# A hybrid decoder layer on one core: gate pieces as tiles of their own, activations behind the high parts, the residual scaled on another engine, 44 ups ahead

## The chip, the core and the metric
The kernel runs on one core of one Trainium2 chip. A time is that of one execution on the device in microseconds; several runs are given by their median. Engines are PE (matrix), DVE (vector), ACT (scalar), POOL (GpSimd) and SP, which only issues transfers here. Each has its own queue and works through it in order.

## What is computed
For 256 tokens of width 2048 (and 16 meta tokens ahead of them, whose output is dropped):
```python
h = layer_norm(concat(meta, x))
proj = h @ w_in                                  # 2048 x 8192
ya = (pool_scale * grouped(multiscale_pool(a), pool_w)) @ pool_proj
yb = (zb * causal_conv(zc * zh)) @ conv_proj
h = layer_norm(ALPHA * h + (g0 * ya + g1 * yb) @ w_out)
q = h @ w_q                                      # 8 heads, two halves of 128
# per head: top 16 of each half's 128 scores, top 16 of their sums -> 16 expert numbers, softmax gate
act = gelu(h . expert_u[idx]);  y = sum(gate * act * expert_v[idx])
out = layer_norm(ALPHA * h + y)
```
There are 16384 experts, 128 blocks of 128. All is float32.

## The kernel before
**Products.** A float32 product is made of rounded parts: `hi`, the value cast to the matrix format, and `lo`, the rest. For each 128x1024 half of a weight tile ACT casts the high part (`whi`, line 95) and DVE or POOL subtracts for the low part (`wlo`, line 74, called by `halves`). PE multiplies the high part with both parts of the tokens and the low part with the high part only (lines 108 and 109, in `mm2`). Weights come in 1 MB tiles named `raw` (line 84), three of them in turn, all issued on SP; the parts have three buffers each.

**Stages.** (1) Layer norm and transposes. (2) Input projection: 64 weight tiles, among them a loop over 8 chunks of the convolution (lines 299 to 320), three tiles a round. In round 1 the residual `res` is scaled by the input norm's row and shifted (lines 319 and 320); it is first read again after the output projection. (3) Output projection, second norm, queries; `q_done` finds the top scores on DVE. (4) The experts are not gathered for the first 224 tokens (`TD`). All 128 blocks are multiplied through instead: an *up* (`up`) multiplies one block of `expert_u` with all tokens and leaves 128 experts x 224 tokens, to which Gelu is applied (line 620); `coef` multiplies it by the gates `G` (line 642), zero for experts not chosen; a *down* (`down`) multiplies the coefficients of four blocks by half the columns of `expert_v` (line 654) and adds to `res` (line 663). The last 32 tokens gather their rows by indirect transfers (`lone_rows`, tile `lone`), a step now and then (a *tick* is half an up or one block of a down).

**Lead.** The first `LEAD` ups run before any down, while the routing ends: `finish(t)` is queued after ups 3 and 6 (`ROUTED`) and goes on by one `yield` per half up; it has the softmax's Exp (line 521). From up 10 on `gates()` builds the gates: a step takes 8 tokens (`GT`), compares indices on DVE (lines 573 to 581), multiplies 16 small matrices on PE (line 592), and ACT copies the result into `wide` (line 594); four steps make a group of 32 tokens (`TG`), which is written to a DRAM tile `spill` (line 597) from POOL's queue. There are 7 groups and 29 calls, spread evenly by `rate` per half up, ending four ups (by the formula) ahead of the lead's end. `G` for four blocks is read back from `spill` for all groups: for the first two fours in `gates` (line 600), for the others by `fetch` (line 738), two slots in turn.

**Order.** The text is not the order on the engines. A planner goes through the program with estimated durations and writes each engine's queue: an engine that is free in its plan takes, of the instructions that are ready in the plan, the one that stands earliest in the text. `tc.high_priority(offset=n)` puts an instruction n places earlier (the parts of weight halves, lines 94 to 98); `tc.issue_after(i)` puts what is issued in its block on the engine of `i` behind `i` in that engine's queue. `late` lets that many Gelus stand back in the text (`gelus`, line 617).

Of the kernel before, what the change touches and what calls it, by code (L numbers as in the profile page):

```python
# [8 lines left out]
F32 = mybir.dt.float32  # L9
# [9 lines left out]
P = 128  # L19
# [19 lines left out]
UAHEAD = 100  # L39
LEAD = 36  # L40
ROUTED = (3, 6)
# [12 lines left out]
def block(ctx, tc, x, meta, w_in, small, pool_w, projs, w_out, wq, keys, eu, eur, ev,  # L54
# [35 lines left out]
    def halves(parts, raw, lo_eng=None, lo_eng1=None, ahead=AHEAD):  # L90
        for s in range(2):
            hi = parts.tile([P, 1024], F32R, name="whi")
            lo = parts.tile([P, 1024], F32R, name="wlo")
            with tc.high_priority(offset=ahead):
                nc.scalar.copy(hi, raw[:, s])  # L95
                eng = lo_eng1 if s and lo_eng1 else lo_eng
                last_lo[0] = lo_part(lo, raw[:, s], hi, eng)
                last_on["pool" if eng is nc.gpsimd else "dve"] = last_lo[0].ins
            yield hi, lo
# [70 lines left out]
    with ExitStack() as pa:  # L170
# [128 lines left out]
        for c in range(NCH):  # L299
            zh = a2.tile([P, T + 2], F32, name="zh", bufs=1)  # L300
            nc.scalar.copy(zh, in_tile(META - 2))
            z = a2.tile([P, T + 2], F32, name="z", bufs=1)
            nc.vector.tensor_tensor(z, in_tile(META - 2), zh, op=OP.mult)
            cv = a2.tile([P, T], F32, name="cv", bufs=1)
            nc.vector.tensor_scalar(cv, z[:, 0:T], conv_w[:, 0, c:c + 1], conv_b[:, c:c + 1],
                                    op0=OP.mult, op1=OP.add)
            for k in (1, 2):
                nc.vector.scalar_tensor_tensor(cv, z[:, k:T + k], conv_w[:, k, c:c + 1], cv,
                                               op0=OP.mult, op1=OP.add)
            zb = a2.tile([P, T], F32, name="zb", bufs=1)  # L310
            both(zb, in_tile(META), T)
            nc.vector.tensor_tensor(cv, zb, cv, op=OP.mult)
            split(yb[:, c, 0], yb[:, c, 1], cv)
            if c == 1:
                with tc.issue_after(last_load[0]):
                    bcast_row(lg, lin_g)
                    bcast_row(lb, lin_b)
                for t in range(NT):
                    nc.gpsimd.tensor_tensor(res[:, t], res[:, t], lg, op=OP.mult)
                    nc.gpsimd.tensor_tensor(res[:, t], res[:, t], lb, op=OP.add)  # L320

# [38 lines left out]
    with ExitStack() as pw:  # L360
# [154 lines left out]
        def finish(t):  # L515
# [3 lines left out]
            for _ in range(3):  # L519
                yield  # L520
            nc.scalar.activation(gt, gt, AF.Exp)
            yield
# [5 lines left out]
            if t == NT - 1:  # L528
# [4 lines left out]
                for n in range(SETS):  # L533
                    hs = slice(n * HEADS // SETS, (n + 1) * HEADS // SETS)
                    to = slice(n * LONE, (n + 1) * LONE)
                    nc.vector.tensor_copy(lone_e[to], rows[ones, hs].rearrange("p h k -> p (h k)"))
                    nc.vector.tensor_copy(lone_g[to], gt[ones, hs].rearrange("p h k -> p (h k)"))
                    nc.sync.dma_start(lone[to], res[ones, t])
            ps = ps_mm()
# [12 lines left out]
    with ExitStack() as pb:  # L552
        lonex = pool(pb, "lonex", 1)
        lone = lonex.tile([P, D], F32, name="lone")
        lone_e = lonex.tile([P, NU], I32, name="lone_e")
# [4 lines left out]
        dram = pb.enter_context(tc.tile_pool(name="dram", bufs=1, space=bass.MemoryType.DRAM))  # L560
        spill = dram.tile([NG, P, NKEY, TG], F32, name="spill")
        p_oh = ExitStack()
# [4 lines left out]
        def gates():  # L567
# [16 lines left out]
            def product(t0, Ag, B):  # L584
# [11 lines left out]
                if o + GT == TG:  # L596
                    nc.gpsimd.dma_start(spill[n], wide[0])
                    for g, eng in ((n - 1, nc.gpsimd), (n if n == NG - 1 else -1, nc.sync)):
                        for b in range(2 if g >= 0 else 0):
                            eng.dma_start(Gs[b][:, g], spill[g, :, b * NB:(b + 1) * NB])  # L600

# [15 lines left out]
        def gelus(left):  # L617
            while len(acts) > left:
                gl = acts.pop(0)
                nc.scalar.activation(gl, gl, AF.Gelu)  # L620

# [114 lines left out]
        def fetch(n):  # L736
            Gs[n] = Gp.tile([P, NG, NB, TG], F32, name="G")
            nc.sync.dma_start(Gs[n], spill[:, :, n * NB:(n + 1) * NB].rearrange("g p i t -> p g i t"))

# [12 lines left out]

        for e in range(LEAD):
            tick(up(e, (nc.gpsimd, nc.gpsimd), UAHEAD, 4 if e <= ROUTED[1] + 2 else 0))
            if e in ROUTED:
                waiting.append(finish(ROUTED.index(e)))
            if e == ROUTED[1] + 3:
                while waiting:
                    step()
                ahead, rate = gates(), (TD // GT + 1) / (2 * (LEAD - 4 - e))  # L760
        for _ in ahead:
            pass
        p_oh.close()
        p_r.close()
        coefp = pool(pb, "coefp", NB + 1)
        lonep = pool(pb, "lonep", 1)
        p_g1 = pb.enter_context(ExitStack())
        rowp = pool(p_g1, "rowp", 2)
# [121 lines left out]
```

## Time and profile before
| | us |
|---|---|
| median of 3 runs (lowest, highest) | 2182.58 (2181.99, 2183.01) |
| profiled execution, its own time | 2188.65 |
| span of the profiled execution | 2186.9 |
| PE busy | 2076.8 |
| DVE, ACT, POOL busy | 1548.2, 1008.9, 586.4 |

PE is busy for 95% of the span, at a mean granted clock of 0.975 (1.00 is the upper of its two levels, 2.4 GHz; the lower is 1.2). The page cuts the span into 40 equal slices of 54.7 us and gives the busy tenths of each. In a row of a window the columns are: from and to, length, and for each engine its busy time and number of instructions, then PE's granted clock, the DMA engines' share and GB/s; PEld is the load of weights, beside PE. A row of a timeline has the start, the duration, the engine, the line, the operation, what is written from what, its shape and count, and in brackets the idle time before it with what ended it. A row of the waits has who waited for whom, the sum, the count and the longest.

### The profile page before, as it was taken

How to read it: one execution, taken by the hardware profiler on the slowest of the kernel's cores; microseconds unless marked ns; L12 is line 12 of the kernel's file. 1: busy time of each engine (PE TensorE's matmuls, PEld its weight loads, DVE VectorE, ACT ScalarE, POOL GpSimd, SP SyncE). 2: the span in 40 equal slices, each digit the busy share in tenths (PEclk: the TensorE clock that was granted, in tenths of full speed). 3: DMA queues.
4: the chain of work that ended last, by engine and by line, in shares of the span. 5: the costliest groups of instructions: out<-in, count | busy, mean ns of one | idle time of the engine just before them, and what ended most of it. 6: DMA issues, size and time to landing. Idle time of an engine off the chain costs nothing.

```text
span 2186.9 us, 29680 instructions
## 1 busy us (share of the span) xinstructions
PE 2076.8 (95%) x11558; PEld 1785.8 (82%) x11558; DVE 1548.2 (71%) x2332; ACT 1008.9 (46%) x1423; POOL 586.4 (27%) x290
## 2 busy tenths in 40 slices
PE   7989999999997787887999999999999999999997
PEld 7989888888886777776888888888888888887775
DVE  7865566666779667755777777776677777678877
ACT  5434545444442454443444444444454444444542
POOL 0110000000073675652323233232333333330001
PEclk9999999999999899898999999999999999999998
DMA  5545555566543345567787877877778787777554
GB/s 196 193 165 183 193 181 187 192 230 229 198 166 122 135 179 199 213 241 245 266 295 260 288 271 265 289 268 285 272 272 284 266 293 261 269 276 250 193 193 154
DMA packets 111452, 498.06 MB, mean 228 GB/s; under 512 B 8320, under 2 KB 35456, under 8 KB 70464
## 3 DMA queue, kind: packets, MB, share of 16 engines
q1 hardware_dynamic: 100704, 413.60, 55.1%
q0 software_dynamic: 10608, 82.58, 9.5%
q8 instruction: 90, 1.47, 0.3%
q14 instruction: 50, 0.41, 0.1%
HBM read 478.32 MB, written 16.78 MB: 226 GB/s over the span
## 4 chain that ended last, share of the span: by engine, by line
PE 55%; DMA 2%; DVE 1%; POOL 0%; issue 0%; ACT 0%; SPq 0%; DVEq 0%; POOLq 0%
PE acc L654 27%; PE mm L108 15%; PE mm L109 7%; PE mm L654 5%; DMA G<-spill 1%; DMA spill<-wide 0%; DVE gl L642 0%; POOL wlo L74 0%; PE mm L592 0%; DVE res L806 0%; DVE res L805 0%; DVE st L140 0%; DVE res L663 0%; ACT whi L95 0%; DVE c_lo L74 0%
## 5 line engine op out<-in xcount | busy, mean ns | idle before, releaser
L95 ACT CAST whi<-raw 128x1024 fp32r<-128x1024 f32 x738 | 771.6, 1048 | 707.1 <-PE mm L108 258.8
L74 DVE TENSOR_TENSOR wlo<-raw,whi 128x1024 fp32r<-128x1024 f32 x554 | 689.6, 1249 | 422.8 <-ACT whi L95 418.4
L108 PE MATMUL mm<-x_hl,whi 128*128 128x448 f32 x2048 | 670.9, 384 | 21.3 <-ACT whi L95 21.3
L74 POOL TENSOR_TENSOR wlo<-raw,whi 128x1024 fp32r<-128x1024 f32 x184 | 463.2, 2525 | 679.5 <-ACT whi L95 344.6
L109 PE MATMUL mm<-x_hl,wlo 128*128 128x224 f32 x2048 | 551.1, 269 | 43.0 <-POOL wlo L74 34.3
L109 PEld LDWEIGHTS mm<-x_hl,wlo 128*128 128x128 f32 x2048 | 401.3, 196 | 49.3 <-POOL wlo L74 38.0
L108 PEld LDWEIGHTS mm<-x_hl,whi 128*128 128x128 f32 x2048 | 394.8, 193 | 56.1 <-ACT whi L95 22.4
L654 PE MATMUL acc<-wlo,c_hi 128*128 128x512 f32 (+1 forms) x864 | 270.2, 394 | 9.5 <-DVE wlo L74 9.5
L654 PE MATMUL acc<-whi,c_lo 128*128 128x512 f32 (+1 forms) x864 | 270.2, 394 | 0.0
L654 PE MATMUL acc<-whi,c_hi 128*128 128x512 f32 (+1 forms) x864 | 269.5, 393 | 0.0
L108 PE MATMUL mm<-h_hl,whi 128*128 128x512 f32 x640 | 226.7, 397 | 0.0
L654 PEld LDWEIGHTS acc<-wlo,c_hi 128*128 128x128 f32 (+1 forms) x864 | 151.0, 175 | 57.7 <-DVE wlo L74 9.9
L654 PEld LDWEIGHTS acc<-whi,c_lo 128*128 128x128 f32 (+1 forms) x864 | 151.5, 175 | 48.4
L109 PE MATMUL mm<-h_hl,wlo 128*128 128x256 f32 x640 | 181.3, 283 | 5.5 <-DVE wlo L74 5.5
L654 PEld LDWEIGHTS acc<-whi,c_hi 128*128 128x128 f32 (+1 forms) x864 | 147.7, 175 | 44.5
L136 POOL TENSOR_TENSOR rstd<-rstd,neghalf 128x1 f32<-128x1 f32 (+1 forms) x7 | 5.8, 826 | 659.3 <-DVE rstd L135 659.3
L663 DVE SCALAR_TENSOR_TENSOR res<-res,acc 128x512 f32<-128x512 f32 x216 | 136.9, 681 | 31.4 <-PE acc L654 28.6
L620 ACT ACTIVATE gl<-gl 128x224 f32<-128x224 f32 x128 | 50.1, 392 | 234.2 <-DVE gl L113 234.2
L108 PEld LDWEIGHTS mm<-h_hl,whi 128*128 128x128 f32 x640 | 121.2, 189 | 27.7
L109 PEld LDWEIGHTS mm<-h_hl,wlo 128*128 128x128 f32 x640 | 121.8, 190 | 5.8 <-DVE wlo L74 5.8
L104 PE MATMUL mm<-h_hl,wlo 128*128 128x258 f32 (+3 forms) x384 | 110.1, 287 | 4.1 <-DVE wlo L74 4.1
L103 PE MATMUL mm<-h_hl,whi 128*128 128x258 f32 (+3 forms) x384 | 111.5, 291 | 0.0
(189 smaller groups left out, 2573.0 us busy)
## 6 DMA issues: line engine op xcount, KB each, us to landing
raw<-in_eu SPq DMA_DIRECT2D x128, 1024.0 KB, 4.9
raw<-in_ev SPq DMA_DIRECT2D x128, 1024.0 KB, 5.4
raw<-in_w_in SPq DMA_DIRECT2D x64, 1024.0 KB, 5.4
raw<-in_projs SPq DMA_DIRECT2D x16, 1024.0 KB, 6.4
raw<-in_w_out SPq DMA_DIRECT2D x16, 1024.0 KB, 5.4
raw<-in_wq SPq DMA_DIRECT2D x16, 1024.0 KB, 4.9
spill<-wide POOLq DMA_DIRECT2D x7, 2048.0 KB, 9.4
G<-spill SPq DMA_DIRECT2D x30, 448.0 KB, 6.7
```

What stands on the lines that cost most here:

```text
L74: return (eng or nc.vector).tensor_tensor(lo, full, hi.bitcast(F32), op=OP.subtract)
L95: nc.scalar.copy(hi, raw[:, s])
L103: nc.tensor.matmul(ps, whi, xlo, start=False, stop=False)
L104: nc.tensor.matmul(ps, wlo, xhi, start=False, stop=last)
L108: nc.tensor.matmul(ps[:, :2 * n].rearrange("p (s t) -> p s t", s=2), whi, xhl, start=first, stop=False)
L109: nc.tensor.matmul(ps[:, :n], wlo, xhl[:, 0], start=False, stop=last)
L136: nc.gpsimd.tensor_tensor(r[:n], r[:n], neghalf[:n], op=OP.pow)
L620: nc.scalar.activation(gl, gl, AF.Gelu)
L654: nc.tensor.matmul(ps[c][:n_t], c_[:, ts], v_[:, c * 512:(c + 1) * 512], start=e == first and n == 0, stop=e == last and n == 2)
L663: nc.vector.scalar_tensor_tensor(r, r, 1.0 if (t, dh, c) in added else ALPHA, ps[c][:n_t], op0=OP.mult, op1=OP.add)
```

## The change
Five things are changed. The DVE scales `res`, in 8 pieces of 512 columns over rounds 1 to 7 instead of four passes of POOL in round 1; the two rows for it are loaded one round earlier. Exp and each Gelu are queued behind the newest high part on ACT, and 3 Gelus stand back through the whole lead. `spill` becomes seven DRAM tiles; in `gates` the reads of a group are queued behind the put of the next; a `fetch` is seven transfers. The lead is 44 ups and the gates end seven ups (by the formula) ahead of its end. `lone` is filled after the lead, from the same rows of `res`, and its tile is made there.
```diff
-LEAD = 36
+LEAD = 44
@@ halves
-                nc.scalar.copy(hi, raw[:, s])
+                last_on["act"] = nc.scalar.copy(hi, raw[:, s]).ins
@@ convolution loop
-            if c == 1:
+            if c == 0:
                 with tc.issue_after(last_load[0]):
                     bcast_row(lg, lin_g)
                     bcast_row(lb, lin_b)
-                for t in range(NT):
-                    nc.gpsimd.tensor_tensor(res[:, t], res[:, t], lg, op=OP.mult)
-                    nc.gpsimd.tensor_tensor(res[:, t], res[:, t], lb, op=OP.add)
+            else:
+                for n in range(8 * (c - 1) // 7, 8 * c // 7):
+                    q = slice(n % 4 * 512, (n % 4 + 1) * 512)
+                    r = res[:, n // 4, q]
+                    with tc.issue_after(last_on["dve"]):
+                        nc.vector.tensor_tensor(r, r, lg[:, q], op=OP.mult)
+                        nc.vector.tensor_tensor(r, r, lb[:, q], op=OP.add)
@@ finish
-            nc.scalar.activation(gt, gt, AF.Exp)
+            with tc.issue_after(last_on["act"]):
+                nc.scalar.activation(gt, gt, AF.Exp)
...
-                    nc.sync.dma_start(lone[to], res[ones, t])
@@ the experts' tiles
-        lone = lonex.tile([P, D], F32, name="lone")
-        spill = dram.tile([NG, P, NKEY, TG], F32, name="spill")
+        spill = [dram.tile([P, NKEY, TG], F32, name=f"spill{n}") for n in range(NG)]
@@ gates
-                    nc.gpsimd.dma_start(spill[n], wide[0])
-                    for g, eng in ((n - 1, nc.gpsimd), (n if n == NG - 1 else -1, nc.sync)):
-                        for b in range(2 if g >= 0 else 0):
-                            eng.dma_start(Gs[b][:, g], spill[g, :, b * NB:(b + 1) * NB])
+                    put = nc.gpsimd.dma_start(spill[n], wide[0])
+                    with tc.issue_after(put.ins):
+                        for g, eng in ((n - 1, nc.gpsimd), (n if n == NG - 1 else -1, nc.sync)):
+                            for b in range(2 if g >= 0 else 0):
+                                eng.dma_start(Gs[b][:, g], spill[g][:, b * NB:(b + 1) * NB])
@@ gelus
-                nc.scalar.activation(gl, gl, AF.Gelu)
+                with tc.issue_after(last_on["act"]):
+                    nc.scalar.activation(gl, gl, AF.Gelu)
@@ fetch
-            nc.sync.dma_start(Gs[n], spill[:, :, n * NB:(n + 1) * NB].rearrange("g p i t -> p g i t"))
+            for g in range(NG):
+                nc.sync.dma_start(Gs[n][:, g], spill[g][:, n * NB:(n + 1) * NB])
@@ the lead
-            tick(up(e, (nc.gpsimd, nc.gpsimd), UAHEAD, 4 if e <= ROUTED[1] + 2 else 0))
+            tick(up(e, (nc.gpsimd, nc.gpsimd), UAHEAD, 3))
...
-                ahead, rate = gates(), (TD // GT + 1) / (2 * (LEAD - 4 - e))
+                ahead, rate = gates(), (TD // GT + 1) / (2 * (LEAD - 7 - e))
         for _ in ahead:
             pass
+        gelus(0)
...
         lonep = pool(pb, "lonep", 1)
+        lone = lonep.tile([P, D], F32, name="lone")
+        for n in range(SETS):
+            nc.sync.dma_start(lone[n * LONE:(n + 1) * LONE], res[P - LONE:, NT - 1])
```

## Rows read from the trace of the kernel before

**Rows 1.** The page's 40 slices of the span: busy tenths of PE.
```profile
PE   7989999999997787887999999999999999999997
```
**Rows 2.** Windows of five stretches, all engines.
```profile
100.00:125.00 25.00, 15.39 (x88) 14.15 (x88) 23.54 (x10) 4.71 (x7) 18.55 (x4) 0.80 0.33 119
150.00:300.00 150.00, 150.00 (x992) 137.73 (x991) 88.51 (x116) 68.85 (x96) 0.00 (x0) 1.00 0.54 185
812.00:970.00 158.00, 130.66 (x966) 120.90 (x964) 106.37 (x168) 73.09 (x122) 102.40 (x58) 0.89 0.59 209
1050.00:1950.00 900.00, 900.00 (x4777) 765.22 (x4776) 649.08 (x769) 433.16 (x599) 293.28 (x142) 1.00 0.78 277
2000.00:2050.00 50.00, 50.00 (x219) 37.92 (x218) 42.89 (x49) 25.73 (x29) 1.44 (x1) 1.00 0.61 207
```
**Rows 3.** Windows, line 109 alone (one per pair of an up): PE, PEld, clock.
```profile
688.00:742.00 54.00, 23.25 (x79) 17.52 (x79) 0.78 0.34 103
740.00:755.00 15.00, 12.34 (x47) 8.90 (x48) 1.00 0.65 218
700.00:790.00 90.00, 48.08 (x170) 35.60 (x170) 0.83 0.39 129
812.00:970.00 158.00, 85.31 (x301) 63.21 (x302) 0.89 0.59 209
970.00:1010.40 40.40, 15.61 (x52) 11.73 (x51) 0.80 0.74 244
```
**Rows 4.** Windows, line 592 alone (matmuls of gate steps): PE, PEld, clock.
```profile
812.00:970.00 158.00, 26.33 (x363) 22.39 (x360) 0.89 0.59 209
```
**Rows 5.** Timeline of POOL and DVE, 99 to 130 us.
```profile
99.13 9.28 POOL L319 TENSOR_TENSOR res<-res,lng 128x2048 f32<-128x2048 f32 x2 [84.16 <-DVE ya L74]
99.46 4.54 DVE L312 TENSOR_TENSOR cv<-zb,cv 128x256 f32<-128x256 f32 x1
...
125.40 1.23 DVE L74 TENSOR_TENSOR wlo<-raw,whi 128x1024 fp32r<-128x1024 f32 x1 [1.79 <-ACT whi L95]
129.79 0.42 DVE L312 TENSOR_TENSOR cv<-zb,cv 128x256 f32<-128x256 f32 x1
```
**Rows 6.** Timeline of ACT, 690 to 800 us: Exp and one Gelu.
```profile
710.16 0.31 ACT L521 ACTIVATE gt<-gt 128x128 f32<-128x128 f32 x1 [15.50 <-DVE gt L518]
...
768.54 0.39 ACT L620 ACTIVATE gl<-gl 128x224 f32<-128x224 f32 x1 [8.61 <-DVE gl L113]
```
**Rows 7.** Timeline of DVE: the adds that empty the first ups' banks.
```profile
713.90 0.38 DVE L113 TENSOR_TENSOR gl<-gl,mm 128x224 f32<-128x224 f32 x1
...
727.51 0.38 DVE L113 TENSOR_TENSOR gl<-gl,mm 128x224 f32<-128x224 f32 x1
...
734.96 0.39 DVE L113 TENSOR_TENSOR gl<-gl,mm 128x224 f32<-128x224 f32 x1
```
**Rows 8.** Waits of the whole span.
```profile
POOL G L600 <- DMA spill<-wide: 41.1, 6, 9.4
```
**Rows 9.** Timeline of POOL: low parts of ups, and reads of gates.
```profile
736.78 19.24 POOL L74 TENSOR_TENSOR wlo<-raw,whi 128x1024 fp32r<-128x1024 f32 x8 [2.46 <-ACT whi L95]
...
948.86 1.11 POOL L600 DMA_DIRECT2D G<-spill  x2 [5.23 <-DMA spill<-wide]
```
**Rows 10.** Timeline of DVE, 940 to 1045 us: first and last run-ahead multiplies.
```profile
973.96 1.90 DVE L642 TENSOR_TENSOR gl<-gl,G 128x224 f32<-128x224 f32 x6 [6.28 <-DMA G<-spill]
...
1007.91 1.30 DVE L642 TENSOR_TENSOR gl<-gl,G 128x224 f32<-128x224 f32 x4 [7.23 <-DMA G<-spill]
```
**Rows 11.** DMA issues: engine, count, KB each, median us to landing.
```profile
G<-spill SPq DMA_DIRECT2D x30, 448.0 KB, 6.7
...
G<-spill POOLq DMA_DIRECT2D x12, 64.0 KB, 2.1
```
**Rows 12.** Timeline of SP in the main loop: a fetch and the next loads.
```profile
1289.87 0.38 SPq L738 DMA_DIRECT2D G<-spill  x1
1291.93 7.28 SPq L84 DMA_DIRECT2D raw<-in_ev  x2
```

## The prediction

> **What bounds the kernel now.** I read the page's slices first: PE is at nine tenths or more almost everywhere, with dents in slices 1 (the start, which the change leaves alone), 3 and 13 to 19 [rows 1]. The windows then say how full PE is where there is no dent: 900.00 of 900 us between 1050 and 1950, at full clock [rows 2]. Nothing that the change does there can give time; it can only take some. So the time to be had is what is lost in the dents, 700 to 1010 us above all, and I size it by counting work. An up is 16 pairs of matmuls (high, then low part); undisturbed, 47 to 48 pairs take 15.0 us [rows 3], so a pair is 0.314 us and an up 5.0 us. A gate step is 16 small matmuls, 0.88 us at full clock by my estimate (0.055 us each, their start distance). Elapsed time less work at that speed is the loss, idle time and low clock together:
> - 700 to 790: 170 pairs are 53.4 us, with 2 us of transposes and first gate products; 34 us lost.
> - 812 to 970: 301 pairs (94.5) and 363 gate matmuls (20.0) [rows 3, 4]; 43 us lost.
> - 970 to 1010.4: 52 pairs (16.3); 24 us lost.
> - 100 to 125: 15.39 of 25 us busy, so 9.6 idle, and the granted clock of 0.80 means 10 us at the lower level, 1.2 GHz [rows 2]. Part of those 10 us is idle anyway, so the clock costs at most 5; I take 3. Together 12.6 us.
> The sum is 114 us, the most that the change can win.
>
> **Residual on DVE.** Before, POOL scales res in four 128x2048 passes, two of them 9.28 us, and is busy 18.55 of these 25 us; a DVE operation beside them takes 4.54 us that alone takes 0.42 [rows 2, 5]. The low parts come late and PE waits. The change takes POOL out of this: 12.6 us back. It adds 16 DVE operations of 128x512. A 128x1024 one takes 1.23 us [rows 5], so about 0.61 each, 9.8 us, over seven rounds of the convolution loop. They are hidden by DVE's own idle time, 61 us between 150 and 300 [rows 2], and stand behind the newest low part, so they delay the next one by 1.2 us at most. Without that cover they cost 9.8 us; below zero they can't go. I take 0. The two row loads go to SP one round earlier, same number, same bytes.
>
> **Exp and Gelu behind the high parts.** ACT is a queue: at 694 it reaches Exp, waits 15.50 us for DVE, and all high parts of the next ups wait behind it; the Gelu at 768.54 does the same for 8.61 us [rows 6]. Now Exp stands behind the high parts of the up traced last (the sixth), and each Gelu behind those of an up three later. The wait itself stays: DVE is late. What is late next is the add that empties an up's PSUM bank, at 713.90, 727.51 and 734.96 for the first three ups [rows 7], and there are four banks. So ups 0 to 3 run through; up 4 starts at about 714.3; up 5 waits for the second add, and its high part also for the Gelu of up 1, which is queued in front of it: 727.9 + 0.4 Gelu + 1.05 high part, so it ends near 735.5; up 6 follows the third add and ends at about 742. That is 7 ups by 742, against 79 pairs, 4.9 ups, before [rows 3]: 10 us. The later stall at 768 (about 8 us) goes, since no high part stands behind a young Gelu any more and two ups fit into the 12 us for which DVE is late. I take 18 of the 34 us. Bounds: 5 (only Exp moves, DVE's adds come later still) and 30 (DVE's adds come earlier in the new order).
>
> **Gate pieces.** POOL puts a group of 32 tokens to the spill, then comes to the reads of the same group and waits until the write has landed, 41.1 us in 6 waits, 9.4 the longest; the row at 948.86 shows one [rows 8, 9]. The low parts of the ups queue behind it. With separate tiles, and the reads behind the next put, a read finds its write landed four steps earlier. The two reads take POOL 1.11 us [rows 9], the put by estimate half of that, 1.7 us per four steps in all. Is another engine late next? The rate falls from 29/46 to 29/56 step per half up, so a step has 1.93 x 2.5 + 0.88 = 5.7 us of PE instead of 4.85. DVE was busy 106.4 us for 22.7 steps, 4.7 each with the adds [rows 2, 4]: 83%. POOL needs 1.93 low parts of 2.4 us (19.24 for 8 [rows 9]) and 0.4: 5.1 us, 89%. Both fit. Of the 43 us I take 39; bounds 25 (POOL's 1.7 us burst shows each time and the last write still blocks SP) and 43.
>
> **Transition and the 44 ups.** When the gates are done, DVE runs ahead: it multiplies all waiting Gelus by their gates, group after group, each group's G fetched by SP into two slots. First multiply 973.96, last of nine groups 1007.91: 34 us [rows 10], and the low parts that the next ups and the first down need on DVE stand between and behind them. That is the 24 us. After, the gates end 6 ups before the lead's end and not 3, so 15 us more of ups, whose low parts are all on POOL, run beside the chain. But 44 ups are eleven groups, and two more cost 34/7 = 4.9 us each. Loss 24 - 15 = 9 if nine groups stand ahead of the first low part on DVE, 19 if eleven: I take 13, a gain of 11; bounds -5 and 21. The eight lead ups have both low parts on POOL, 4.8 of 5.0 us: no cost, and 1.6 us if each of the 16 stretches by a tenth. The four lone loads move from the routing (SP has the same issues there and here) to this place, behind the release of the gate tiles; they are needed only by the first gathered row, so 0, and 5 us if SP is held by them.
>
> A fetch is now seven issues of 64 KB instead of one of 448 KB. The single one lands in 6.7 us, a 64 KB read from POOL in 2.1 [rows 11]. If the seven overlap, a fetch takes 7 x 0.38 + 2.1 = 4.8 us; one after another, 14.7. I keep 6.7, between them, for the chain. The Trainium skill (DMA: Bandwidth & Descriptors, Anatomy of one DMA) gives each DMA on the POOL path a fixed 2.0 us and a part that goes with the bytes, and puts most of the fixed part down to the receipt of the write; by that the pieces overlap, 64 KB is 2.15 us (the trace: 2.1) and 448 KB only 3.0, where the trace has 6.7; by its figures the sum below would come out some 7 us lower. In the main loop the fetch is 2.26 us more of SP per group. SP issues a fetch at 1289.87 and then waits until 1291.93 for a raw slot [rows 12], so 1.7 us of it fit into that wait and the rest into the lead of three raw tiles: 0.
>
> The lone rows take as many ticks as before; 64 of them now lie in the downs-only end, where DVE is busy 42.89 of 50 us with PE at 50.00 [rows 2]: 0.
>
> **Sum.** 12.6 + 18 + 39 + 11 = 80.6, say 81 us. The profiled execution took 2188.65 us (span 2186.9), 6 us over the median of the runs; from its time 2107.6, and by the same difference 2182.58 - 81 = 2101.6 as the median. About 0.2%, 4.4 us, is what a measurement can tell from no change.
>
> **Rivals.**
> - Nearly all of it goes (0.20): DVE's adds are placed earlier, the chain overlaps. 12.6 + 26 + 42 + 21 = 102: 2081. For it: DVE has idle time in the new gate stage. Against: the adds at 727.51 and 734.96 are late by DVE's own queue, with no idle time ahead of them [rows 7], whatever ACT does.
> - The pieces land one after another in the chain (0.15). 8 us more per fetch, two in flight, so 4 more per group; seven groups 62 us instead of 34; the transition loses 44 instead of 24: 12.6 + 18 + 39 - 20 = 50: 2133. The Trainium skill's fixed price per DMA (same page and section) speaks for it, if it is paid in turn. Against: the two POOL reads of a group are issued side by side and still land in 2.1 us [rows 11].
> - The reads still wait (0.07), because what they wait for is not the tile but the queue's newest write: 12.6 + 18 + 0 + 11 = 42: 2141. For it: the wait named in the rows is the write. Against: it is the write of the same group.
> - Slower (0.05): the pieces land in turn in the main loop too, and hold back the raw loads behind them in SP's queue. 30 fetches x (8 - 1.7 - c), where c is how early raw tiles lie ready. With c = 3 that is 99 us, against 50 won: 2232. It decides from c = 4.6 us. Against: PE is full for 900 us with no wait on a raw load, and three tiles are in flight.
> - My forecast: 0.53.
>
> The range holds the forecast, the first rival and most of the second: 2073 to 2138, with 2 in 10 outside. Faster by over 0.2%: all but the slower rival and a little of the third's tail, 0.94; within 0.2% 0.01; slower 0.05.
>
> **What would show it.** Right: 100 to 125 at PE 25 of 25; no POOL wait on the spill between 800 and 980 and PE over 0.95 there; ACT still waiting for DVE near 715 to 735, but no wait of Exp over 2 us; a stall of 10 to 20 us once, at the first main-loop up, with DVE waiting for G; from there PE full. Wrong: PE idle in the main loop behind a raw load; low parts on POOL late after each put; a transition as long as before; or DVE full through the gate stage.

## The result and the profile after

The changed kernel takes 2130.34 us (median of 4 runs, 2129.3 to 2131.58) beside 2182.8 us for the one before (2181.99 to 2183.15, same chip): a ratio of 0.976, 95% interval 0.9744 to 0.9777. The forecast was 2101.6 us; the gain is 52 us where 81 were forecast, and the time lies in the range, 8 us under its upper end. The profiled execution took 2131.58 us (span 2129.8, mean granted clock 0.986).

The page's slices of PE show what is left of the dents in [rows 1]:
```profile
PE   7999999999999699997999999999999999999997
```
Counted from 1, slices 3, 13 and 15 to 18 are at nine tenths or more now; a slice is 53.2 us long. Two dents remain, slice 14 (692 to 745 us) and slice 19 (958 to 1012). The windows size them (columns as in the windows of before):
```profile
100.00:150.00 50.00, 50.00 (x373) 47.93 (x372) 33.06 (x43) 20.65 (x27) 0.00 (x0) 1.00 0.52 180
...
690.00:700.00 10.00, 3.32 (x22) 2.92 (x20) 10.00 (x22) 2.34 (x2) 4.20 (x2) 0.82 0.62 211
700.00:710.00 10.00, 2.53 (x9) 2.39 (x10) 10.00 (x60) 1.57 (x3) 1.24 (x1) 0.50 0.01 2
...
765.00:938.00 173.00, 173.00 (x1384) 163.51 (x1383) 133.77 (x212) 101.32 (x170) 146.74 (x76) 1.00 0.74 268
938.00:1016.00 78.00, 57.33 (x277) 49.15 (x276) 42.52 (x75) 26.52 (x42) 28.30 (x13) 0.85 0.75 234
...
1100.00:1700.00 600.00, 600.00 (x3180) 509.70 (x3179) 431.85 (x522) 289.33 (x402) 195.51 (x94) 1.00 0.79 277
```
The stretch in which POOL scaled the residual before [rows 2] and the stretch of the gates (765 to 938) are full at clock 1.00, and so is the main loop. In the first dent it is DVE that is busy without a gap (10.00 of 10, twice) while PE stands. To count work as before, the windows of line 109 alone:
```profile
690.00:765.00 75.00, 42.31 (x151) 31.48 (x151) 0.84 0.39 133
765.00:938.00 173.00, 122.78 (x468) 88.98 (x467) 1.00 0.74 268
938.00:1016.00 78.00, 32.90 (x114) 24.50 (x113) 0.85 0.75 234
```
At 0.314 us a pair, 0.055 us a gate matmul (448 of them from 765 to 938) and 0.23 us a matmul of a down (50 from 938 to 1016), the losses are:

| stretch | before, us lost | after, us lost | gain | forecast |
|---|---|---|---|---|
| residual (100 to 125; first up starts 674.3, was 688.0) | 12.6 | about 0 | 13.7 | 12.6 |
| routing (before 700 to 790, after 690 to 765) | 34 | 75 - 47.4 - 1.4 = 26 | 8 | 18 |
| gates (before 812 to 970, after 765 to 938) | 43 | 173 - 147.0 - 24.6 = 1 | 42 | 39 |
| transition (before 970 to 1016, after 938 to 1016) | 46 - 16.3 - 4.4 = 25.3 | 78 - 35.8 - 11.5 = 30.7 | -5.4 | 11 |

The 1.4 us are transposes. The gains add up to 58, where the two profiled executions differ by 57.1 (2188.65 and 2131.58). The medians differ by 52.5, 4.6 less: the profiled execution of before lay 6 us over its median, this one 1.2. The forecast took a gain counted in the profiled execution from the median of the runs.

The waits show the change of the limits. PE, 650 to 765 us, and DVE, 930 to 1016 us (who waited for whom, sum, count, longest):
```profile
PE mm L108 <- DVE gl L113: 16.6, 2, 14.1
```
```profile
DVE gl L647 <- DMA G<-spill: 38.0, 9, 8.9
```
No wait of POOL for a write of the spill, 41.1 us before [rows 8], is left between 765 and 938. The timeline of ACT from 690 to 765 us and that of DVE's adds that empty the banks answer to [rows 6, 7]:
```profile
707.36 0.39 ACT L625 ACTIVATE gl<-gl 128x224 f32<-128x224 f32 x1 [14.19 <-DVE gl L113]
...
724.61 0.31 ACT L526 ACTIVATE gt<-gt 128x128 f32<-128x128 f32 x1
```
```profile
706.96 0.37 DVE L113 TENSOR_TENSOR gl<-gl,mm 128x224 f32<-128x224 f32 x1
720.37 0.38 DVE L113 TENSOR_TENSOR gl<-gl,mm 128x224 f32<-128x224 f32 x1
727.82 0.68 DVE L113 TENSOR_TENSOR gl<-gl,mm 128x224 f32<-128x224 f32 x2
```
Exp now starts with no idle time before it. What ACT and PE wait for is the add of the first up, at 706.96. The transition is the chain of multiplies on DVE, to be held against [rows 10]:
```profile
937.56 2.21 DVE L647 TENSOR_TENSOR gl<-gl,G 128x224 f32<-128x224 f32 x7 [7.42 <-DMA G<-spill]
...
952.54 5.67 DVE L647 TENSOR_TENSOR gl<-gl,G 128x224 f32<-128x224 f32 x4 [8.94 <-DMA G<-spill]
...
1009.94 0.98 DVE L647 TENSOR_TENSOR gl<-gl,G 128x224 f32<-128x224 f32 x3
```
From the first multiply to the last one of the lead it runs 72 us for eleven groups, where nine took 34.

### The profile page after: what moved, and what is told of

The parts are those of the page before. It is cut to its first block, busy times and chain, and to the rows that moved or that the text cites. A ratio compares the mean times of both kernels' runs of the same rounds, so it can differ in the third digit from the quotient of the medians.

```text
span 2129.8 us, 29941 instructions
## 1 busy us (share of the span) xinstructions
PE 2059.4 (97%) x11558; PEld 1771.9 (83%) x11558; DVE 1543.6 (72%) x2340; ACT 1009.4 (47%) x1424; POOL 587.9 (28%) x294
## 4 chain that ended last, share of the span: by engine, by line
PE 89%; DVE 7%; DMA 2%; issue 1%; POOL 1%; SPq 0%; ACT 0%; POOLq 0%; DVEq 0%; ACTq 0%
PE mm L108 28%; PE acc L659 26%; PE mm L109 14%; PE mm L659 6%; PE mm L103 2%; PE mm L102 2%; PE mm L104 2%; PE acc L116 2%; PE acc L117 2%; PE acc L118 2%; DMA G<-spill 1%; PE mm L595 1%; POOL wlo L74 1%; PE acc L219 0%; DVE eq L514 0%
## 5 line engine op out<-in xcount | busy, mean ns | idle before, releaser
L74 DVE TENSOR_TENSOR wlo<-raw,whi 128x1024 fp32r<-128x1024 f32 x546 | 672.1, 1235 | 401.6 <-ACT whi L95 397.8
L108 PE MATMUL mm<-x_hl,whi 128*128 128x448 f32 x2048 | 660.4, 380 | 20.2 <-DVE gl L113 16.6
L74 POOL TENSOR_TENSOR wlo<-raw,whi 128x1024 fp32r<-128x1024 f32 x192 | 481.5, 2512 | 625.9 <-ACT whi L95 311.0
L109 PE MATMUL mm<-x_hl,wlo 128*128 128x224 f32 x2048 | 545.1, 266 | 14.9 <-POOL wlo L74 8.5
L109 PEld LDWEIGHTS mm<-x_hl,wlo 128*128 128x128 f32 x2048 | 396.0, 193 | 18.9 <-POOL wlo L74 10.1
L659 PE MATMUL acc<-wlo,c_hi 128*128 128x512 f32 (+1 forms) x832 | 260.7, 395 | 8.2 <-DVE wlo L74 8.2
L659 PE MATMUL acc<-whi,c_lo 128*128 128x512 f32 (+1 forms) x832 | 260.7, 394 | 0.0
L659 PE MATMUL acc<-whi,c_hi 128*128 128x512 f32 (+1 forms) x832 | 260.1, 394 | 0.0
L659 PEld LDWEIGHTS acc<-wlo,c_hi 128*128 128x128 f32 (+1 forms) x832 | 145.5, 175 | 55.3 <-DVE wlo L74 9.4
L108 PEld LDWEIGHTS mm<-h_hl,whi 128*128 128x128 f32 x640 | 120.2, 188 | 27.2
L103 PE MATMUL mm<-h_hl,whi 128*128 128x258 f32 (+3 forms) x384 | 110.5, 288 | 0.0
L102 PE MATMUL mm<-h_hl,whi 128*128 128x258 f32 (+3 forms) x384 | 109.4, 286 | 0.0
```

The costliest lines, as they stand in the source:

```text
L74: return (eng or nc.vector).tensor_tensor(lo, full, hi.bitcast(F32), op=OP.subtract)
L102: nc.tensor.matmul(ps, whi, xhi, start=first, stop=False)
L103: nc.tensor.matmul(ps, whi, xlo, start=False, stop=False)
L108: nc.tensor.matmul(ps[:, :2 * n].rearrange("p (s t) -> p s t", s=2), whi, xhl, start=first, stop=False)
L109: nc.tensor.matmul(ps[:, :n], wlo, xhl[:, 0], start=False, stop=last)
L659: nc.tensor.matmul(ps[c][:n_t], c_[:, ts], v_[:, c * 512:(c + 1) * 512], start=e == first and n == 0, stop=e == last and n == 2)
```

## The experiments

Each kernel is the changed one with the edit shown, timed in three rounds beside the kernel before; ratios are to the kernel before, with 95% intervals. The runs stand on three chips, where the kernel before took 2183.2, 2184.7 and 2184.0 us; an interval is some 3.5 us to either side, so a difference of 2 or 3 us to the changed kernel is not told from none.

**The residual back on POOL.** `e1_pool_residual`
```diff
-            if c == 0:
+            if c == 1:
...
-            else:
-                for n in range(8 * (c - 1) // 7, 8 * c // 7):
...
+                for t in range(NT):
+                    nc.gpsimd.tensor_tensor(res[:, t], res[:, t], lg, op=OP.mult)
+                    nc.gpsimd.tensor_tensor(res[:, t], res[:, t], lb, op=OP.add)
```


> The changed kernel with one part undone: POOL scales the residual again, in round 1. My count gives this part 13.7 us, so 2130.3 + 13.7 = 2144 us, with a window of 25 us around 105 to 125 that has PE idle for some 9 us. Rival: the up starts earlier for another reason (the row loads one round earlier, the planner's order), then 2130 within 3 us.

Measured: 2146.12 us, ratio 0.9828 (0.9811 to 0.9844), 15.8 us more than the changed kernel. The window of 100 to 125 us is that of before again [rows 2], the clock too:
```profile
100.00:125.00 25.00, 15.32 (x88) 14.08 (x87) 23.40 (x11) 4.79 (x7) 18.35 (x4) 0.80 0.31 115
```
The term of the residual is confirmed. Its 16 operations on DVE cost PE nothing that shows: in the changed kernel PE is busy 550.00 of 550 us between 100 and 650.

**Exp and Gelu where the planner puts them.** `e2_no_act_order`
```diff
-            with tc.issue_after(last_on["act"]):
-                nc.scalar.activation(gt, gt, AF.Exp)
+            nc.scalar.activation(gt, gt, AF.Exp)
...
-                with tc.issue_after(last_on["act"]):
-                    nc.scalar.activation(gl, gl, AF.Gelu)
+                nc.scalar.activation(gl, gl, AF.Gelu)
```


> The changed kernel without the two orders on ACT: Exp and Gelu go where the planner puts them, late stays 3. My count gives the part 8 us (26 us lost in the routing instead of 34): 2138 us, and an Exp that waits some 15 us for DVE. Rival: DVE's late adds and the PSUM banks set the routing whatever ACT does, then 2130 within 3 us.

Measured: 2136.35 us, ratio 0.9781 (0.9764 to 0.9797), 6.0 us more. Exp waits 15.3 us for DVE again, and PE waits for the high part behind it (waits of PE, 690 to 765 us):
```profile
PE mm L108 <- ACT whi L95: 19.6, 3, 10.6
```
The order does what it says and is worth a third of the 18 us taken for it. It also has a price, which this run shows: without it the first add starts at 701.12, 5.8 us earlier than with it, though the ups start at the same time (674.07 and 674.30).

**More banks, and more late Gelus.** Two runs ask what binds the routing now. The first gives every other early up an accumulator bank that is idle then, and lets seven Gelus stand back up to up 11; the second does the latter alone. `e7_banks_and_late` and `e8_late_only`
```diff
-            ps = ps_mm()
+            ps = ps_acc(e // 2 % 2, e // 4 % 2) if e < 9 and e % 2 else ps_mm()
...
-            tick(up(e, (nc.gpsimd, nc.gpsimd), UAHEAD, 3))
+            tick(up(e, (nc.gpsimd, nc.gpsimd), UAHEAD, 7 if e <= 11 else 3))
```


> The changed kernel with eight PSUM banks for the first nine ups (every second one takes a bank of the accumulators, idle there) and seven Gelus standing back up to up 11. Theory: the routing's 26 us are DVE's late adds, reached through the banks and through the Gelu that waits on ACT; with both relieved PE goes on through ups 3 to 6: 10 to 18 us back, 2112 to 2120 us. Rival: DVE's backlog delays something else that PE needs next (transposes, gate steps), then less than 4 us, 2126 to 2131.

> The changed kernel with seven Gelus standing back up to up 11, four banks as they are. Theory: PE's 14 us wait at 693 is for a bank, so ACT's freedom alone gives little: 2126 to 2131 us, and the wait of PE for DVE's add stays over 10 us. Rival: ACT's queue is what binds, then the same gain as with banks, 2112 to 2120.

Measured: 2127.42 us with both (ratio 0.9736, 0.972 to 0.9753), 2.9 us less than the changed kernel; 2139.0 us with the late Gelus alone (0.979, 0.9771 to 0.9808), 8.7 more. With late Gelus alone the wait for the bank stands, 15.2 us at the longest, so the bank is what stops PE, as that run's theory had it. Its time was missed all the same (2126 to 2131 expected): PE's waits for DVE's adds grow to 27.2 us in three, from 16.6 in two. With the banks PE runs through, and then stands one step later (windows and waits of PE, the run with both):
```profile
680.00:710.00 30.00, 27.75 (x178) 25.99 (x176) 30.00 (x72) 11.75 (x17) 24.44 (x10) 1.00 0.59 207
710.00:740.00 30.00, 14.54 (x56) 13.00 (x57) 28.08 (x105) 8.75 (x15) 11.75 (x5) 0.66 0.20 71
```
```profile
PE mm L545 <- DVE gt L531: 12.9, 1, 12.9
```
The transposes of the softmax (line 545) wait for the same engine. DVE is busy 58.08 of these 60 us: its backlog is the limit of the routing, and who waits for it only changes its name. The rival of that run holds.

**Reads not queued behind the next put.** `e4_reads_free`
```diff
-                    with tc.issue_after(put.ins):
-                        for g, eng in ((n - 1, nc.gpsimd), (n if n == NG - 1 else -1, nc.sync)):
-                            for b in range(2 if g >= 0 else 0):
+                    for g, eng in ((n - 1, nc.gpsimd), (n if n == NG - 1 else -1, nc.sync)):
+                        for b in range(2 if g >= 0 else 0):
...
```


> The changed kernel with separate tiles, but the reads not queued behind the next put. Theory: the planner puts them back right behind their own write and POOL waits for it to land: most of the 43 us of the gate stage comes back, 2165 to 2175 us. Rival: the tiles alone were enough, 2130 within 3 us.

Measured: 2165.8 us, ratio 0.9919 (0.9902 to 0.9935), 35.5 us more. With seven tiles but the reads where the planner puts them, POOL's wait is back (waits, whole span):
```profile
POOL G L603 <- DMA spill<-wide: 39.1, 6, 9.3
```

**One spill tile and one transfer for a fetch, the reads still behind the next put.** `e3_one_spill_tile`
```diff
-        spill = [dram.tile([P, NKEY, TG], F32, name=f"spill{n}") for n in range(NG)]
+        spill = dram.tile([NG, P, NKEY, TG], F32, name="spill")
...
-            for g in range(NG):
-                nc.sync.dma_start(Gs[n][:, g], spill[g][:, n * NB:(n + 1) * NB])
+            nc.sync.dma_start(Gs[n], spill[:, :, n * NB:(n + 1) * NB].rearrange("g p i t -> p g i t"))
```


> The changed kernel with one DRAM tile for all gate groups and one transfer per fetch again; the reads stay queued behind the next put. Theory: the place in the queue does the work and the separate tiles do nothing for it, so the gate stage stays full; and a fetch in one piece lets the run of multiplies after the gates go faster, so 2120 to 2128 us. Rival 1: a read waits for whatever was last written to its tile, so the tiles are needed: POOL waits 40 us for the spill again and the time is 2165 to 2175. Rival 2: pieces cost nothing, 2130 within 3 us.

Measured: 2126.81 us, ratio 0.9738 (0.9722 to 0.9754), 3.5 us less than the changed kernel. The gates' stretch is just as full:
```profile
765.00:935.00 170.00, 170.00 (x1363) 160.55 (x1363) 133.40 (x210) 102.04 (x170) 146.00 (x77) 1.00 0.73 265
```
So the order of the queue is enough for the gates' gain; separate tiles are not needed for it, and without the order they don't give it. What the seven transfers of a fetch cost is less sure: the two intervals overlap. The chain of multiplies shows it more plainly. Its 44th multiply, the last of the lead's, starts at 984.01, the first at 937.92: 46 us instead of 72. But the transition loses 26.1 us still (117 pairs and 66 matmuls of downs between 938 and 1016), 4.6 less (timeline of DVE and window, this run):
```profile
984.01 0.39 DVE L647 TENSOR_TENSOR gl<-gl,G 128x224 f32<-128x224 f32 x1 [0.46 <-ACT gl L625]
```
```profile
938.00:1016.00 78.00, 58.55 (x300) 51.32 (x299) 44.70 (x80) 29.16 (x47) 29.02 (x13) 0.87 0.79 255
```

**A lead of 36.** `e5_lead36`
```diff
-LEAD = 44
+LEAD = 36
...
-                ahead, rate = gates(), (TD // GT + 1) / (2 * (LEAD - 7 - e))
+                ahead, rate = gates(), (TD // GT + 1) / (2 * (LEAD - 4 - e))
```


> The changed kernel with the lead of 36 ups and the gates spread as before (29 calls over 23 ups); all else as changed. Theory: the loss after the gates is the run of multiplies that DVE makes ahead of its time, nine groups instead of eleven, with 15 us less of ups beside it, so that loss stays near 30 us; and DVE needs 4.7 of the 4.85 us of a step, so a few us appear in the gate stage: 2130 to 2140 us. Rival: 44 ups are what makes the gate stage full, then PE waits in it again and the time is over 2150. Rival 2: two groups less make the run shorter and nothing else changes, 2120.

Measured: 2129.9 us, ratio 0.9747 (0.973 to 0.9763): no difference, at the lower edge of the theory. Its loss after the gates is there: 30 us between 900 and 1016 (168 pairs, 144 matmuls of downs), in a chain that takes 62 us for its nine groups. The few us that it put on the gate stage are not: the shorter stretch holds PE full although DVE is at 97% in it:
```profile
770.00:900.00 130.00, 130.00 (x1093) 122.67 (x1091) 126.44 (x200) 81.10 (x138) 108.80 (x58) 1.00 0.75 273
```

**The multiplies in their turn.** Is the transition the run-ahead of the multiplies? Here each stands on DVE behind the newest low part. `e6_coef_in_turn`
```diff
-            nc.vector.tensor_tensor(glv, glv, Gs[e // NB][:, :, e % NB], op=OP.mult)
+            with tc.issue_after(last_on["dve"]):
+                nc.vector.tensor_tensor(glv, glv, Gs[e // NB][:, :, e % NB], op=OP.mult)
```


> The changed kernel with each multiply by the gates queued on DVE behind the newest low part, so that DVE can't run ahead through the groups. Theory: the 31 us lost between 938 and 1016 are this run, waited out on DVE with SP's fetches in front of the raw loads; without it some 25 us come back: 2100 to 2110 us, no wait of DVE for G over 3 us. Rival: the loss is raw loads held on SP behind the last write and the lone loads, then less than 5 us change, 2126 to 2130. Rival 2: multiplies in turn come too late for their down in the main loop, some 1 us per group, then 2125 or slower.

Measured: 2120.14 us, ratio 0.9701 (0.9684 to 0.9717), 10.2 us less than the changed kernel and the fastest of all runs; 2100 to 2110 was expected. Windows of this run:
```profile
938.00:1016.00 78.00, 75.36 (x405) 66.16 (x406) 39.12 (x52) 37.21 (x57) 35.32 (x17) 0.96 0.78 270
...
1850.00:1900.00 50.00, 48.40 (x210) 36.30 (x209) 43.62 (x55) 20.21 (x25) 4.33 (x3) 1.00 0.77 268
...
2000.00:2050.00 50.00, 43.88 (x173) 32.26 (x172) 37.62 (x50) 23.05 (x26) 0.00 (x0) 0.90 0.54 169
```
144 pairs and 117 matmuls of downs stand between 938 and 1016, 45.2 + 26.9 us: 5.9 us lost instead of 30.7. That part of the theory holds in full. But 14 of the 24.8 us are given back after 1850 us, where only downs are left and the changed kernel is full: 9.3 us idle up to 2050, with the granted clock down to 0.90, and that is the cause of its second rival, in the end with downs alone. PE's waits from 1016 us on are on the parts of the coefficients, and their sum is those 9.3:
```profile
PE acc L660 <- DVE c_lo L74: 5.0, 3, 1.8
PE acc L660 <- ACT c_hi L77: 4.3, 1, 4.3
```

**In turn only as long as ups are left.** To keep the one and undo the other, the order is dropped after key group 20 of 32. Three more runs add to it one spill tile, later loads of the lone rows, and the extra banks, each on top of the last. `e9_coef_in_turn_while_ups`, `e10_and_one_spill_tile`, `e11_and_lone_loads_later`, `e12_and_a_bank_more`
```diff
+            turn = tc.issue_after(last_on["dve"]) if n_up < NKEY else ExitStack()
+            with turn:
+                nc.vector.tensor_tensor(glv, glv, Gs[e // NB][:, :, e % NB], op=OP.mult)
...
...
+                if e0 == dh == 0:
+                    for n in range(SETS):
+                        nc.sync.dma_start(lone[n * LONE:(n + 1) * LONE], res[P - LONE:, NT - 1])
+                    lone_work, lone_rate = lone_rows(), (4 * NU + 4) / LONE_TICKS
```
The second hunk, which stands ahead of the first down, is in the last two of the four runs only; the tile and the banks are edited as shown above.

> The multiply by the gates goes to DVE in its turn only as long as first products (ups) are left, up to key group 20 of 32; after that as in the changed kernel. Theory: the multiplies in turn gained 24.8 us between 938 and 1016 (loss 30.7 to 5.9 us) and lost about 9 us of idle and 5 us of clock after 1850 us, where only second products are left and the multiply in turn comes too late for the next group. With the one kept and the other undone the time is 2120 - 14 = about 2106, between 2103 and 2111, and the end from 1850 us is full as in the changed kernel (50 of 50). Rival: the loss after 1850 us comes from something else that the earlier transition brings (transfers, the backlog of DVE); then the end stays as in the run with all multiplies in turn, 2118 to 2122.

Measured: 2131.0 us, ratio 0.9751 (0.9735 to 0.9768). Neither the theory (2103 to 2111) nor its rival (2118 to 2122) holds. The end is full, as the theory had it; but the loss turns up at a third place, where the order is dropped (windows and waits of DVE of this run, the latter for 1740 to 1840):
```profile
938.00:1016.00 78.00, 75.28 (x411) 65.95 (x412) 39.56 (x53) 38.38 (x58) 35.33 (x17) 0.98 0.80 274
...
1700.00:1800.00 100.00, 93.33 (x486) 79.33 (x485) 65.73 (x83) 43.04 (x61) 31.83 (x15) 0.97 0.75 262
1800.00:1850.00 50.00, 39.78 (x178) 30.66 (x177) 33.65 (x56) 16.76 (x24) 11.81 (x5) 0.92 0.76 252
...
1950.00:2000.00 50.00, 50.00 (x218) 37.92 (x217) 42.65 (x50) 22.92 (x29) 4.32 (x3) 1.00 0.73 252
```
```profile
DVE gl L649 <- DMA G<-spill: 26.2, 6, 7.8
```
44 multiplies, the eleven groups that are left, run between 1754 and 1845: the chain of the transition, moved by 800 us. From 938 to 1016 there are 411 matmuls instead of 277, 134 more; from 1700 to 1850 there are 664, where the changed kernel has 798 (538 + 260), 134 fewer, at its 0.188 us each 25 us. In both kernels the run-ahead is paid once, where DVE is let go.

> As the run before, and the gate pieces lie in one memory tile and each group of four key blocks is fetched by one DMA instead of seven. Theory: the seven pieces stretched the run-ahead chain of multiplies at the transition; with the multiplies in turn that chain is gone, and of the 3.5 us that one tile gave by itself little is left: 0 to 2 us under the run before, 2103 to 2108. Rival: the seven issues hold SP's queue ahead of the weight loads, whatever DVE's order is; then the 3.5 us come in full, 2101 to 2104.

> As the run before, and the four loads of the lone rows (and the work on them) are issued two first products later. Theory: at 934 to 943 us these loads stand in SP's queue between weight loads; TensorE waits there 1.7 and 2.0 us for split weights and then runs 7 us at granted clocks of 0.54 and 0.77; with the loads later, both go: 3 to 6 us under the run before. Rival: the queue is held by the last gate piece's reads, which wait for the write (3.5 us of wait), and the weight load behind it is late all the same: within 1.5 us of the run before.

> As the run before, and the first ups alternate with accumulator banks that are idle then, with seven Gelus left late up to up 11 (this alone gave 2.9 us on the changed kernel). Theory: the stall by the banks after the third up goes and a part of it comes back at the routing product that waits for DVE's backlog, as there: 2 to 4 us under the run before. Rival: the routing's lost time only moves into the gates' stretch; no difference within 1 us.

Measured: 2135.82 (ratio 0.9779, 0.9763 to 0.9796), 2137.84 (0.9785, 0.9768 to 0.9801) and 2135.03 us (0.9771, 0.9755 to 0.9788). The first two expectations missed. One tile, 3.5 us faster by itself, is 4.8 slower here: 644 matmuls from 1700 to 1850, 20 fewer, and in the routing, whose code is the same, PE is busy 92.28 us from 650 to 765 instead of 95.86. So a difference of this size also comes from the planner's new order, and neither run shows a price of the transfer alone. The run with the lone loads later doesn't test its theory. They stand later in the text, but the planner put them at the same place in SP's queue (timelines of SP, the run before it and this one), and so SP's wait for the last write (waits of SP, 925 to 960 us) and PE's waits for the parts of the weights, 1.7 and 2.0 us, are as they were:
```profile
934.12 1.23 SPq L777 DMA_DIRECT2D lone<-res  x2
```
```profile
934.88 1.23 SPq L792 DMA_DIRECT2D lone<-res  x2
```
```profile
SPq L604 <- DMA spill<-wide: 3.6, 1, 3.6
```
Whether the lone loads or the last write hold up the weights stays open. The banks moved the stall from 693 to the softmax's transposes again (a wait of 13.5 us for line 531); 2.8 us less, within the 2 to 4 expected, but no more than the interval can tell.

## Why the prediction was right in direction and 29 us off

**Read rightly.** Where the time could come from (four dents), and that nothing was to be had or lost in the main loop: the seven issues of a fetch cost nothing there, 600.00 of 600 us. The residual: 12.6 us forecast, 13.7 by the start of the first up, 15.8 by the run that undoes it. The gates: 39 forecast, 42 seen, 35.5 by the run that frees the reads. The cause there was named a little wrongly: the step gave separate tiles and the order together the credit, and the order alone is enough. Routing and gates came out within their bounds, the transition (-5.4) just past its lower one. The rival in which the reads still wait fell; it describes the kernel without the order.

**Routing, 18 forecast, 8 seen (6 by the run that undoes the order).** The failed step: "So ups 0 to 3 run through". Three run through, 48 pairs by 700 us; the fourth finds no bank, and PE stops at 693.3. The step counted four banks for the ups, but the routing's own products take theirs from the same four: between the first ups PE writes four transposes at 679.29 and eight products of scores at 682.24 (lines 461 and 468) to them. And the first adds came at 706.96, 720.37 and 727.82, 7 us earlier than before, while the ups start 13.7 earlier: by the clock of this stage DVE is 7 us later than forecast. The step took DVE's lateness as given, and the change itself adds to it. Since Exp no longer holds up ACT, the high parts of four ups come at once and POOL makes eight low parts in a row, where it made four; the run without the order on ACT makes four again. While POOL is at them, several small operations of DVE take as long as a low part (POOL in the changed kernel and in the run without the order, then one operation of DVE, changed and before):
```profile
674.47 11.78 POOL L74 TENSOR_TENSOR wlo<-raw,whi 128x1024 fp32r<-128x1024 f32 x5 [17.54 <-PE acc L118]
686.93 7.38 POOL L74 TENSOR_TENSOR wlo<-raw,whi 128x1024 fp32r<-128x1024 f32 x3 [0.67 <-ACT whi L95]
```
```profile
674.24 9.44 POOL L74 TENSOR_TENSOR wlo<-raw,whi 128x1024 fp32r<-128x1024 f32 x4 [17.55 <-PE acc L118]
```
```profile
692.04 2.35 DVE L500 SCALAR_TENSOR_TENSOR far<-rc 128x64 f32<-128x64 f32 x1
```
```profile
699.62 0.20 DVE L496 SCALAR_TENSOR_TENSOR far<-rc 128x64 f32<-128x64 f32 x1
```
From the last reduction (line 516, before 512) ahead of the first add to that add, DVE takes 27.3 us before, 28.5 without the order, 34.1 here and 39.7 with more banks; POOL is busy 11.8, 11.8, 19.0 and 31.7 us of it. The prediction had read this effect in the residual (4.54 us for 0.42) and did not ask for it here. ACT's wait changed its name, from Exp to the Gelu of the first up (14.19 us), and of the later stall half stays (a Gelu waits 4.11 us for DVE at 756).

**Transition, 11 forecast, 5 lost.** 30.7 us were lost where the prediction took 13; of its own signs of being wrong, "a transition as long as before" is the one that came. The 15 us more of ups beside the chain were there: 41 ups, 655 pairs, are done by 938, when the first multiply starts, so three of the lead are left, where before less than one was. The failed step is the sum: "Loss 24 - 15 = 9 if nine groups stand ahead of the first low part on DVE, 19 if eleven", a loss that goes by the length of the chain, less the ups beside it. It doesn't go by that length. The chain takes 34 us in the kernel before, 46 with a single transfer per fetch, 62 with a lead of 36 and 72 here; lost are 25.3, 26.1, 30 and 30.7 us. So the price of a group, "two more cost 34/7 = 4.9 us each", is off here (6.6) and about right with the single transfer (4.2), and the loss is twice the forecast with either. SP's timeline shows what the step left out. First the changed kernel, then the one with the multiplies in turn:
```profile
951.94 0.33 SPq L84 DMA_DIRECT2D raw<-in_eu  x1
952.46 7.99 SPq L744 DMA_DIRECT2D G<-spill  x12
960.55 0.39 SPq L84 DMA_DIRECT2D raw<-in_ev  x1
960.99 8.86 SPq L744 DMA_DIRECT2D G<-spill  x12
969.95 0.38 SPq L84 DMA_DIRECT2D raw<-in_ev  x1
970.37 8.57 SPq L744 DMA_DIRECT2D G<-spill  x13
979.05 0.38 SPq L84 DMA_DIRECT2D raw<-in_eu  x1
```
```profile
955.11 5.77 SPq L84 DMA_DIRECT2D raw<-in_ev  x2
965.73 4.34 SPq L84 DMA_DIRECT2D raw<-in_eu  x2
974.34 7.59 SPq L84 DMA_DIRECT2D raw<-in_ev  x2
986.19 4.67 SPq L84 DMA_DIRECT2D raw<-in_eu  x2
```
While DVE runs ahead, SP issues fetch after fetch, some twelve issues of 0.4 us in a row, with 6.6 us of waits until the multiplies give a slot of G free, and one weight load between them: a load every 9 us, where an up uses one in 5.0. With the single transfer the loads are as rare, five from 946.5 to 987.4, and there SP also waits until low parts of POOL and DVE give a raw tile free (21.0 and 15.1 us between 938 and 1016). With the multiplies in turn the loads come in pairs, one every 5 us or so. This is the prediction's rival of the slower kernel, raw loads held back behind fetches, in the one stage where SP has no slack; the prediction looked for it in the main loop only. How far the late loads and the low parts behind DVE's waits each count is not parted, since both go with the run-ahead. That 44 ups pay nothing is shown by the run with 36; the bound of -5 was the right number.

**The pieces.** The rival in which they land one after another gave 2133, 3 us from the measured time, and is wrong all the same. It is nearly right on the chain, which is 26 us longer with the pieces, but with a single transfer 3.5 us come back, not the 31 between its time and the forecast. Two short terms, routing and transition, added up to its price. The upper end of the range was drawn for this rival, so that the time lies inside it is in part luck. Why the chain is longer with pieces isn't shown: a piece lands in 4.7 us (median of 212), the single 448 KB in 6.5. By the fit of the Trainium skill (DMA: Bandwidth & Descriptors, Anatomy of one DMA), which is for transfers on the POOL path, 64 KB would take 2.15 us and 448 KB 3.0, both estimates. The trace of before agrees for 64 KB on POOL's queue (2.1 [rows 11]); on SP's queue, where a fetch is issued, the runs show neither figure.

**What is shown of the transition.** That the run-ahead costs it: put the multiplies in turn and 25 us go; drop the order later and 25 us come back at that place. What isn't shown is a version with neither the chain nor the loss at the end; letting the multiplies run ahead by one group at a time was not tried. The best kernel measured is the one with all of them in turn, 2120.1 us.

## What to carry to other kernels

A queue that works in order turns a plan's optimism into a wait: when an engine may take work early whose data come from a slow transfer, it stands in front of the transfer with the urgent work behind it; pin such work behind the newest urgent instruction, and look for the next place where the pin ends. Before pricing an order on one engine, look whether the engine that it waits for has any gap: if it is busy 58 of 60 us, a reordering moves most of the wait, and work that the new order starts earlier on a third engine can make that engine later still. And when a measured time agrees with a rival, undo that rival's cause alone before believing it.

## What the runs showed of the hardware that was not expected

- While POOL makes low parts of 128x1024 (2.4 us each), operations of DVE on 128 columns or fewer take 2.2 to 2.5 us where the same shape takes 0.15 to 0.25 us elsewhere in the trace of the changed kernel; five of them stand between 679 and 695.
- A 64 KB read of the spill issued on POOL's queue right behind a 2 MB write lands after 8.1 us (median of 12), where it took 2.1 us after the wait for the write [rows 11] and takes 2.4 us in the run that frees the reads. It costs nothing here, since the G of the first groups is needed later.
- DVE at 97% busy (126.44 of 130 us) did not hold up PE in the gates' stretch of the run with 36 ups, while at 97% in the routing (58.08 of 60 us) it did: there the work that PE waited for stood behind the routing's in DVE's queue.
- A stall of PE costs more than its length in the trace: after the waits of 1.7 and 2.0 us around 936 to 941 us in the run with all multiplies in turn, the granted clock is 0.54 from 940 to 945 and 0.77 from 945 to 950, so PE ran nearly all of the first 5 us and about half of the next at the lower level (1.2 GHz) and not the upper (1.00, 2.4 GHz).
